# One scatter for four experts through rotating row blocks, in a two-layer expert kernel with a fixed TensorE order

## The chip, the cores and the metric

The kernel runs on one core of a Trainium2 chip, as one program. The metric is the device time of one execution, in microseconds (us); lower is better. All arithmetic on activations and weights is in float32, some of it as pairs of reduced-precision halves.

The engines by their short names: PE (TensorE) multiplies matrices into PSUM, its accumulation memory, and PEld is its weight load; DVE (VectorE) and ACT (ScalarE) do elementwise work; SP (SyncE) issues the transfers. Each engine takes its instructions in the order in which they stand in its queue.

## The reference

Two layers over 256 latent tokens and 256 context tokens of width 1024. In each, a mixer (attention, windowed attention, short convolution), and then 16 routed experts of which each picks its own 32 tokens of each stream. In the second layer only the latent stream goes on to the experts.

```python
def expert_choice_ffn(h, w_router, w_g, w_u, w_d):
    B, n, D = h.shape
    cap = CAPACITY_FACTOR * n // N_EXPERTS                  # 32
    logits = jnp.einsum('bnd,de->ben', h, w_router, preferred_element_type=jnp.float32)
    aff = jax.nn.softmax(logits, axis=1)
    gate, idx = lax.top_k(aff, cap)
    bi = jnp.arange(B)[:, None, None]
    xs = h[bi, idx]
    a = jnp.einsum('becd,edf->becf', xs, w_g)
    u = jnp.einsum('becd,edf->becf', xs, w_u)
    y = jnp.einsum('becf,efd->becd', jax.nn.silu(a) * u, w_d)
    return jnp.zeros_like(h).at[bi, idx].add(y * gate[..., None].astype(y.dtype))

def reference(...):
    for l in range(DEPTH):                                  # 2
        ...
        x = x + gt1 * latent_mixer(...)
        h2 = modulate(rmsnorm(x, g_ffn[l]), sh2, sc2)
        x = x + gt2 * expert_choice_ffn(h2, w_router[l], w_e_gate[l], w_e_up[l], w_e_down[l])
        ...                                                 # the same for the context stream, not in the last layer
    return x
```

## The kernel before

Weights are streamed. `Arena` holds 21 slots of 1 MB (128 partitions x 2048 float32). Loads stand in one queue in the order of `load_mixer` and `load_experts`; SP issues each into the slot that was given back longest ago, and waits there until the last reader of that slot is done. `limit` caps how many tiles may be loaded and not yet used up. An expert has 12 such tiles: `("g", l, e, q)` and `("u", l, e, q)` for the gate and up weights of rows 256 q and on, q from 0 to 3, and `("d", l, e, q)` for the down weights. Expert 15's come in halves of 512 KB.

`experts(l, last, lg)` runs one layer's experts; `last` is layer 1. The number of streams `ns` is 2 in layer 0 and 1 in layer 1, so an expert has NC = 64 rows in layer 0 (32 of each stream) and 32 in layer 1. Routing leaves `pos` (for each token and expert its slot number from 1 to 32, or 0) and the gates (`PA[:, 1]`). Then, expert by expert:

- `gather(g)` builds the one-hot tile `OH` of experts 4g to 4g+3 and multiplies the tokens by it (tile `xg` in PSUM); ACT and DVE bring it to `XS`, modulated. It is called once for four experts, at e = 4g - 2.
- `gate_up(e, q)` multiplies XS by the gate and up tiles into two `gu` tiles in PSUM. In layer 0 each matmul fills 64 columns of the array, and a gate matmul and an up matmul that stand next to each other lie in its two halves; in layer 1 four lie beside each other.
- ACT copies the `gu` tiles out, PE transposes them (`guT`), ACT and DVE make `aT` = silu(gate) x up.
- `down` multiplies aT by the down tiles into `py`, in row blocks of 32, and DVE multiplies `py` by the residual gate into `ys`.
- `spread(e)` builds the way back, `SP`: a matmul (`sp`) copies the expert's row of slot numbers and gates to all partitions, and DVE compares it with the slot number of each partition.
- The scatter (`sc`) multiplies SP by ys, and DVE adds the result to the stream X. In layer 0 it follows every second expert: two experts share the 128 rows, with two partial sums for each of their 64-row blocks. In layer 1 one expert fills all 128 rows with four partial sums, and the scatter follows every expert.

A scheduler sets the order of each engine's instructions from the program's dependencies and its own cost estimates, on PE too. PSUM buffers: four `mm` (gu, guT, sp), one `tp`, one `po`, and one `ps` of two banks (py, and xg of the later gathers).

Of the kernel before, what the change touches and what calls it, by code (L numbers as in the profile page):

```python
# [23 lines left out]
NE = 16  # L24
HID = 1024
CAP = 32
# [63 lines left out]
def hybrid_kernel(ctx, tc, x, c, cx, c_ctx, w_ada, b_ada, g_mix, g_ffn, w_in, qg_a, kg_a, qg_b, kg_b, sink_b,  # L90
# [149 lines left out]
    slotid = const.tile([128, 1], F32, name="slotid")  # L240
    scr = epool.tile([128, CAP], F32, name="scr")
    DVE.scalar_tensor_tensor(scr, slots, 1.0, sel2, op0=OP.mult, op1=OP.mult, accum_out=slotid)
# [772 lines left out]
    def experts(l, last, lg):  # L1015
# [15 lines left out]
        PA = pool.tile([64, 2, 256], F32, name="PA")  # L1031
# [33 lines left out]
        DVE.tensor_tensor(out=av, in0=av, in1=sm.unsqueeze(3).to_broadcast(full), op=OP.mult)  # L1065
        gap(True)
# [23 lines left out]
        def gather(g, mid=None):  # L1090

            if last:

                i, XS = None, gtt[l, 2][1][:, 0].rearrange("p (d e c) -> p d e c", d=8, e=4) if g % 2 else \
                    pool.tile([128, 8, 4, NC], F32, name="XS", tag="XS", bufs=1)
            else:
                i, XS = ar.take([128, 8, 4, NC], F32, "XS")
            XG[g] = (i, XS)

            OH = pool.tile([128, 2 * ns, 4, CAP], F32, name="OH", tag="OH", bufs=1)  # L1100
            for t in tiles:
                DVE.tensor_tensor(out=OH[:, t], in0=pos[:, t, 4 * g:4 * g + 4].unsqueeze(2).to_broadcast([128, 4, CAP]),
                                  in1=slots.unsqueeze(1).to_broadcast([128, 4, CAP]), op=OP.is_equal)
                if g == 0:

                    ACT.activation(OH[:, t], OH[:, t], AF.Copy, scale=nst[:, 3, t:t + 1])
            for h in range(2):
                for s in range(ns):
                    pt = (ptp, ppo)[(h + s) % 2]([128, 4, 128], "xg") if g == 0 else pss([128, 4, 128], "xg")
                    for j in range(4):  # L1110
                        for t in range(2):
                            PE.matmul(pt[:, j, :], (Y if g else X)(2 * s + t)[:, feats(4 * h + j)],  # L1112
                                      OH[:, 2 * s + t].rearrange("p e c -> p (e c)"), start=(t == 0), stop=(t == 1))
                    for j in range(4):
                        d = 4 * h + j
                        o, i_ = XS[:, d, :, 32 * s:32 * s + 32], pt[:, j, :].rearrange("p (e c) -> p e c", e=4)
                        a, b = mod[:, l, 3, s, d:d + 1], mod[:, l, 2, s, d:d + 1]
                        if j % 2:
                            DVE.tensor_scalar(o, i_, a, b, op0=OP.mult, op1=OP.add)  # L1119
                        else:  # L1120
                            ACT.activation(o, i_, AF.Identity, scale=a, bias=b)
                if h == 0 and mid:
                    mid()

        def spread(e):

            se = pool.tile([64, 128], F32, name="se", tag="af", bufs=1)
            n = 128 // ns
            for s in range(ns):
                DVE.tensor_copy(se[0:NR, n * s:n * s + n],  # L1130
                                ident[0:NR, 32 * place(e, s) + e:32 * place(e, s) + e + 1].to_broadcast([NR, n]))
            ps = pmm([128, 512], "sp")
            PE.matmul(ps, se[0:NR], PA[0:NR].rearrange("p a n -> p (a n)"), start=True, stop=True)  # L1133
            af = pool.tile([128, 256], F32, name="af", tag="af", bufs=1)
            ACT.activation(af, ps[:, 256:512], AF.Copy)  # L1135
            if e % ns == 0:
# [174 lines left out]
```

## Time and profile before

| | |
|---|---|
| median of three runs | 1847.61 us (1846.89 to 1850.54) |
| the profiled execution | 1850.58 us, of which the profile's span is 1848.8 |
| mean granted TensorE clock | 0.983 |
| PE busy over the span | 1699.3 us (92%) |
| DVE, ACT busy | 773.6 (42%), 500.5 (27%) |
| bytes moved | 533.79 MB, mean 289 GB/s |
| layer 0's experts | from 556.2 to 1084.3 us |
| layer 1's experts, first gate and up matmuls on | from about 1403 us to the end |

The profiled execution lies 3 us above the median, so a sum made against its span is carried over to the median as a difference. Busy time of PE includes the drain of each run of matmuls, so matmuls that lie beside each other in the array are counted once. The chain of waits follows the work that ended last back from the end: each row is a start, a length and what ran; "issue" is a small gap at the start of an instruction. A matmul in float32 stands as two records, and some records are missing from a trace. The share of DMA is the mean busy share of the 16 DMA engines.

### The profile page before, as it was taken

Reading aid. Unit: us, or ns where it says so; the run is one execution under the profiler, and the core shown is the slowest. Engines: PE = TensorE matmul, PEld = TensorE weight load, DVE = VectorE, ACT = ScalarE, POOL = GpSimd, SP = SyncE. Lnnn points to the kernel's source line nnn. Section 1 sums busy time; section 2 is a strip of 40 time slices with the busy share of each in tenths; the row PEclk is TensorE's granted clock in tenths of the full one; section 3 lists DMA queues with packets and bytes.
Section 4 is the critical chain, followed back from the end, with each engine's and each line's share of the span. In section 5 each row is a group of like instructions: output and inputs, shape, how many; then the busy total and the mean of one; then the engine's idle time right before and its main releaser. Section 6 shows DMA issues by size and latency. Waiting matters only on the chain.

```text
span 1848.8 us, 23239 instructions
## 1 busy us (share of the span) xinstructions
PE 1699.3 (92%) x9198; PEld 935.9 (51%) x9198; DVE 773.6 (42%) x1766; ACT 500.5 (27%) x1089; POOL 0.6 (0%) x6
## 2 busy tenths in 40 slices
PE   7999999999999999899899989999999987778776
PEld 4886666778764333433433337878973322112111
DVE  4787864344542231231221256987653221212111
ACT  4564543223322101101101055655542000000000
POOL 0000000000000000000000000000000000000000
PEclk9999999999999999999999999999999999989999
DMA  9201116655878979989789992235788999999998
GB/s 345 99 27 45 49 66 220 218 166 160 318 294 340 420 294 420 383 362 419 311 359 419 408 365 86 92 92 161 229 337 351 419 420 419 420 420 419 420 420 340
DMA packets 131777, 533.79 MB, mean 289 GB/s; under 512 B 12452, under 2 KB 21076, under 8 KB 85588
## 3 DMA queue, kind: packets, MB, share of 16 engines
q1 hardware_dynamic: 129024, 529.90, 74.0%
q10 hardware_dynamic: 2644, 2.40, 0.4%
q8 instruction: 73, 1.20, 0.3%
q14 instruction: 36, 0.29, 0.0%
HBM read 531.21 MB, written 1.05 MB: 288 GB/s over the span
## 4 chain that ended last, share of the span: by engine, by line
PE 70%; DMA 23%; DVE 3%; ACT 2%; issue 1%; ACTq 0%; SPq 0%; DVEq 0%
DMA s<-in_w_e_up_dram 15%; PE gu L1163 14%; DMA s<-in_w_e_down_dram 8%; PE pf L436 7%; PE pf L437 7%; PE pf L438 7%; PE py L1227 7%; PE sc L1254 3%; PE O L834 3%; PE xg L1112 2%; PE S L772 2%; PE ada L303 2%; PE PTp L808 2%; PE pt L436 2%; PE pt L438 2%; PE pt L437 2%
## 5 line engine op out<-in xcount | busy, mean ns | idle before, releaser
L1163 PE MATMUL gu<-s,s 128*64 128x512 f32 (+1 forms) x1536 | 341.1, 602 | 26.1 <-DMA s<-in_w_e_up_dram 20.8
L437 PE MATMUL pf<-s,wh 128*128 128x512 f32 (+1 forms) x768 | 263.2, 343 | 0.0
L436 PE MATMUL pf<-s,wh 128*128 128x512 f32 (+1 forms) x768 | 262.1, 342 | 0.0
L438 PE MATMUL pf<-s,wl 128*128 128x512 f32 (+1 forms) x768 | 261.6, 342 | 0.0
L467 DVE TENSOR_TENSOR wl<-s,wh 128x512 fp32r<-128x512 f32 x272 | 186.1, 688 | 156.4 <-ACT wh L466 138.2
L466 ACT ACTIVATE wh<-s 128x512 fp32r<-128x512 f32 x272 | 170.5, 630 | 276.3 <-PE pf L437 189.5
L1227 PE MATMUL py<-s,aT 128*32 128x512 f32 x1536 | 200.1, 616 | 33.1 <-DMA s<-in_w_e_down_dram 14.9
L1163 PEld LDWEIGHTS gu<-s,s 128*64 128x64 f32 (+1 forms) x1536 | 99.8, 127 | 249.3 <-issue 182.6
L436 PEld LDWEIGHTS pf<-s,wh 128*128 128x128 f32 x768 | 145.4, 189 | 22.7 <-issue 5.2
L1245 DVE TENSOR_TENSOR ys<-py,s 64x512 f32<-64x512 f32 (+1 forms) x96 | 64.8, 688 | 212.2 <-PE py L1227 201.7
L438 PEld LDWEIGHTS pf<-s,wl 128*128 128x128 f32 x768 | 145.3, 190 | 14.9 <-issue 1.8
L437 PEld LDWEIGHTS pf<-s,wh 128*128 128x128 f32 x768 | 145.6, 190 | 13.9 <-issue 0.7
L1254 PE MATMUL sc<-ys,SP 128*128 128x512 f32 x256 | 124.6, 618 | 17.8 <-DVE ys L1245 17.6
L1227 PEld LDWEIGHTS py<-s,aT 128*32 128x32 f32 x1536 | 52.0, 112 | 159.2 <-issue 95.7
L1213 DVE TENSOR_TENSOR aT<-aT,guT 128x256 f32<-128x256 f32 x48 | 20.0, 420 | 257.1 <-ACT aT L1212 256.6
L1186 ACT ACTIVATE gu<-gu 128x512 f32<-128x512 f32 x48 | 28.5, 596 | 348.4 <-PE gu L1163 348.4
L1135 ACT ACTIVATE af<-sp 128x256 f32<-128x256 f32 x32 | 12.2, 382 | 403.5 <-PE sp L1133 403.5
L1257 DVE TENSOR_TENSOR s<-s,sc 128x512 f32<-128x512 f32 x128 | 87.8, 687 | 37.6 <-PE sc L1254 37.3
L1254 PEld LDWEIGHTS sc<-ys,SP 128*128 128x128 f32 x256 | 40.9, 188 | 104.2 <-DVE s L1257 47.7
L1163 PE MATMUL gu<-s,XS 128*32 128x512 f32 x512 | 80.9, 627 | 11.2 <-DMA s<-in_w_e_up_dram 9.2
L1140 DVE SCALAR_TENSOR_TENSOR SP<-sp,slotid,af 64x256 f32<-64x256 f32 (+1 forms) x48 | 23.2, 484 | 140.0 <-ACT af L1135 139.7
L1112 PE MATMUL xg<-OH,s 128*128 128x128 f32 x384 | 58.3, 309 | 17.7 <-DVE s L1119 14.1
(203 smaller groups left out, 1854.1 us busy)
## 6 DMA issues: line engine op xcount, KB each, us to landing
s<-in_w_e_gate_dram SPq DMA_DIRECT2D x120, 1024.0 KB, 19.0
s<-in_w_e_up_dram SPq DMA_DIRECT2D x120, 1024.0 KB, 16.5
s<-in_w_e_down_dram SPq DMA_DIRECT2D x120, 1024.0 KB, 15.2
s<-in_w_ada_dram SPq DMA_DIRECT2D x48, 1024.0 KB, 10.9
s<-in_w_in_dram SPq DMA_DIRECT2D x46, 1024.0 KB, 7.9
s<-in_w_branch_dram SPq DMA_DIRECT2D x16, 512.0 KB, 10.3
s<-in_w_out_dram SPq DMA_DIRECT2D x8, 1024.0 KB, 7.6
s<-in_w_e_gate_dram SPq DMA_DIRECT2D x16, 512.0 KB
```

The lines of the kernel that those rows point to most:

```text
L436: PE.matmul(ps, lh, rh, start=start, stop=False)
L437: PE.matmul(ps, lh, rl, start=False, stop=False)
L438: PE.matmul(ps, ll, rh, start=False, stop=stop)
L466: ACT.activation(hi, w[:, kk, :], AF.Copy)
L467: DVE.tensor_tensor(out=lo, in0=w[:, kk, :], in1=hi.bitcast(F32), op=OP.subtract)
L834: PE.matmul(O[64 * kv:64 * kv + 64], v[:, k0 + kt, c0:c0 + 64], ipt[kv][1][:, kt].rearrange("p g q -> p (g q)"), start=(kt == 0), stop=(kt ...
L1112: PE.matmul(pt[:, j, :], (Y if g else X)(2 * s + t)[:, feats(4 * h + j)], OH[:, 2 * s + t].rearrange("p e c -> p (e c)"), start=(t == 0), ...
L1163: PE.matmul(gps[fh % nf][r0:r0 + NC], XG[e // 4][1][:, k, e % 4, :], w[a][:, k % 2, 512 * fh:512 * fh + 512], start=(k == 0), stop=(k == 7))
L1227: PE.matmul(py[r0:r0 + 32, h, :], aT[:, ff, 32 * s:32 * s + 32], rhs, start=(ff < n // 32), stop=(ff >= 8 - n // 32))
L1245: DVE.tensor_tensor(out=ys[place(e, i)][r, hs_], in0=py[r, h, :], in1=g2[place(e, i)][r, hs_], op=OP.mult)
L1254: PE.matmul(po[s], back["now"][s][:, ts_], ys[s][:, hs_], start=True, stop=True)
L1257: DVE.tensor_tensor(out=o, in0=o, in1=po[s], op=OP.add)
```

## The change

In layer 0, four experts share one scatter. `block(e, s, h)` = (e + s + 2h) mod 4 names the row block of 32 in which expert e of a group of four has its rows of stream s for half h of the width. `down` in layer 0 goes over both halves and both streams for each 128-row slice of the hidden dimension, so that four neighbouring matmuls have four row blocks; each block now holds one whole sum, and both halves of an expert lie in one bank of `py` (bank e mod 2). `evac` brings the four blocks to `ys`, and `scatter` runs once for four experts, after the last gate and up matmul of the next expert; in layer 1 it runs after that of the next expert too, once for each expert.

`spread` and its matmul are gone. In layer 0 `one_hot` also makes `OG`, the one-hot times the gates with its first three experts repeated, and `way_back` transposes four-expert windows of it on PE, one window for each of two halves and four token tiles; in layer 1 it builds the gated one-hot `four` of one expert and transposes that.

The gather is split in halves, in two alternating PSUM buffers (`tp`, `po`). `gate_up` takes `ks`, so that half of a tile pair can be multiplied: two of the four k-slices' matmuls of the next expert's first pair stand before `guT` and two after it. The load queue has that first pair ahead of this expert's down tiles. In the expert loop PE's instructions stand in the order of the program (`manual_schedule`); the other engines' order stays with the scheduler.

PE in layer 0, around the scatter of a pair of experts before (gu: gate and up matmuls with their weight tile and XS, py: down, sc: scatter; the numbers are those of buffers):

```order
L1227 MATMUL py<-s_4834,aT 32x512 x8
L1163 MATMUL gu<-s_4854,s_4638 64x512
L1163 MATMUL gu<-s_4844,s_4638 64x512
L1254 MATMUL sc_4984<-ys,SP 128x512
L1254 MATMUL sc_4983<-ys,SP 128x512
L1163 MATMUL gu<-s_4854,s_4638 64x512
L1163 MATMUL gu<-s_4844,s_4638 64x512
L1254 MATMUL sc_4989<-ys,SP 128x512
L1254 MATMUL sc_4990<-ys,SP 128x512
L1254 MATMUL sc_4997<-ys,SP 128x512
```

Here gate and up matmuls of the next expert stand one by one between the scatter's. And PE in layer 0 now, around the scatter of the first four experts, which stands in expert 4:

```order
L1183 MATMUL gu<-s_5182,s_5025 64x512
L1216 MATMUL sc<-ys,SP 128x512 x8
L1183 MATMUL gu<-s_5192,s_5025 64x512
L1183 MATMUL gu<-s_5194,s_5025 64x512
L1183 MATMUL gu<-s_5192,s_5025 64x512
L1183 MATMUL gu<-s_5194,s_5025 64x512
L1275 MATMUL guT<-ident,gu 128x128 x8
L1183 MATMUL gu<-s_5192,s_5025 64x512
L1183 MATMUL gu<-s_5194,s_5025 64x512
L1183 MATMUL gu<-s_5192,s_5025 64x512
L1183 MATMUL gu<-s_5194,s_5025 64x512
L1308 MATMUL py<-s_5224,aT 32x512 x8
```

The scatter has moved behind this expert's own gate and up matmuls, the next expert's first pair stands on both sides of guT, and gate and up alternate without a break.

PE at the end of layer 1 (expert 15) before:

```order
L1163 MATMUL gu<-s_12163,s_7303 32x512
L1209 MATMUL guT<-ident,gu 128x128 x4
L1227 MATMUL py<-s_12166,aT 32x512 x4
L1227 MATMUL py<-s_12177,aT 32x512 x4
L1254 MATMUL sc_12297<-ys,SP 128x512
L1254 MATMUL sc_12301<-ys,SP 128x512
```

The transposes follow the last gate and up matmul. The same place now, with OGT the transposed one-hot of `way_back`:

```order
L1183 MATMUL gu<-s_11941,s_7097 32x512
L1216 MATMUL sc<-ys,SP 128x512 x4
L1156 MATMUL OGT<-ident,four 128x128 x2
L1275 MATMUL guT<-ident,gu 128x128 x4
L1232 MATMUL py<-s_11944,aT 32x512 x4
L1232 MATMUL py<-s_11955,aT 32x512 x4
L1216 MATMUL sc<-ys,SP 128x512 x2
```

Expert 14's scatter and expert 15's two transposes have come between the last gate and up matmul and guT. The diff, cut to its core:

```diff
     def load_experts(l):
+        def up(e, q):
+            for nm, w in (("g", w_e_gate), ("u", w_e_up)):
+                rows((nm, l, e, q), w[l, e], q, 2 if e == NE - 1 else 1)
+
+        up(0, 0)
         for e in range(NE):
 
             parts = 2 if e == NE - 1 else 1
-            for q in range(4):
-                for nm, w in (("g", w_e_gate), ("u", w_e_up)):
-                    rows((nm, l, e, q), w[l, e], q, parts)
+            for q in range(1, 4):
+                up(e, q)
+            if e + 1 < NE:
+                up(e + 1, 0)
...
+        aff = pool.tile([128, 2 * ns, NE], F32, name="aff")
+        DVE.tensor_copy(aff.rearrange("p (s t) e -> p t s e", t=2), av)
...
+        def one_hot(g):
...
+            OG = None if last else pool.tile([128, 4, 7, CAP], F32, name="OG", tag="OG", bufs=1)
+            hot[g] = (OH, OG)
...
+            for b0, n in () if last else ((0, 4), (4, 3)):
+                DVE.tensor_tensor(out=OG[:, :, b0:b0 + n], in0=OH[:, :, 0:n],
+                                  in1=aff[:, :, 4 * g:4 * g + n].unsqueeze(3).to_broadcast([128, 2 * ns, n, CAP]),
+                                  op=OP.mult)
...
+        def gather(g, h):
+            OH, XS = hot[g][0], XG[g][1]
+            for s in range(ns):
+                pt = (ptp, ppo)[(h + s) % 2]([128, 4, 128], "xg")
...
+        def block(e, s, h):
+            return (e + s + 2 * h) % 4
+        def way_back(e):
+            if last:
+                pt = ptp([128, 2, 128], "OGT")
+                four = pool.tile([128, 2, 4, CAP], F32, name="four", tag="four", bufs=1)
+                for t in range(2):
+                    DVE.scalar_tensor_tensor(four[:, t], slots.unsqueeze(1).to_broadcast([128, 4, CAP]),
+                                             pos[:, t, e:e + 1],
+                                             aff[:, t, e:e + 1].unsqueeze(2).to_broadcast([128, 4, CAP]),
+                                             op0=OP.is_equal, op1=OP.mult)
+                    PE.transpose(pt[:, t, :], four[:, t].rearrange("p e c -> p (e c)"), ident)
+                back[e] = pool.tile([128, 2, 128], F32, name="SP", tag="SP", bufs=2)
+                ACT.activation(back[e], pt, AF.Copy)
+                return
+            OG = hot[e // 4][1]
+            back[e // 4] = pool.tile([128, 2, 4, 128], F32, name="SP", tag="SP", bufs=1)
             for h in range(2):
+                pt = (ptp, ppo)[h]([128, 4, 128], "OGT")
+                for t in tiles:
+                    o = block(0, 4 - t // 2, -h) % 4
+                    PE.transpose(pt[:, t, :], OG[:, t, o:o + 4].rearrange("p e c -> p (e c)"), ident)
+                ACT.activation(back[e // 4][:, h], pt, AF.Copy)
...
-        def spread(e):
...
+        def gate_up(e, q, ks=(0, 1)):
...
+        def evac(e, py, h):
+            hs_ = slice(512 * h, 512 * h + 512)
+            if last:
+                DVE.tensor_tensor(out=ys[0][:, hs_], in0=py[:, h, :], in1=g2[0][:, hs_], op=OP.mult)
+                return
+            for s in range(ns):
+                r = slice(32 * block(e, s, h), 32 * block(e, s, h) + 32)
+                DVE.tensor_tensor(out=ys[s][r, hs_], in0=py[r, e % 2, :], in1=g2[s][r, hs_], op=OP.mult)
+
+        def scatter(e, h):
+            hs_ = slice(512 * h, 512 * h + 512)
+            for t in range(2):
+                for s in range(ns):
+                    po = (ptp, ppo)[(s if ns == 2 else t)]([128, 512], "sc")
+                    w = back[e][:, t] if last else back[e // 4][:, h, 2 * s + t]
+                    PE.matmul(po, w, ys[s][:, hs_], start=True, stop=True)
+                    o = X(2 * s + t)[:, hs_]
+                    DVE.tensor_tensor(out=o, in0=o, in1=po, op=OP.add)
...
+        order = tc.manual_schedule(engines={mybir.EngineType.PE})
+        order.__enter__()
         for e in range(NE):
...
+            if e and (last or e % 4 == 0):
+                scatter(e - 1, 0)
+                scatter(e - 1, 1)
+            if last or e % 4 == 1:
+                way_back(e)
+            if last or e % 4 == 0:
                 ys = [pool.tile([128, D], F32, name="ys", tag=f"ys{s}", bufs=1) for s in range(ns)]
-            if e + 1 < NE:
-                spread(e + 1)
-            if e % 4 == 2 and e + 2 < NE:
-                gather(e // 4 + 1)
+            ahead = e % 4 == 2 and e + 2 < NE
+            if ahead:
+                one_hot(e // 4 + 1)
+                gather(e // 4 + 1, 0)
...
+            if e + 1 < NE:
+                gate_up(e + 1, 0, (0,))
...
+            if ahead:
+                gather(e // 4 + 1, 1)
+            if e + 1 < NE:
+                gate_up(e + 1, 0, (1,))
+            if last or e % 2 == 0:
+                py = pss([128, 2, 512], "py")
...
+                for q in range(4):
+                    w = ar.get(("d", l, e, q))
                     for ff in range(2 * q, 2 * q + 2):
+                        for h in range(2):
+                            for s in range(ns):
+                                r0 = 32 * block(e, s, h)
+                                PE.matmul(py[r0:r0 + 32, e % 2, :], aT[:, ff, 32 * s:32 * s + 32],
+                                          w[:, ff % 2, 512 * h:512 * h + 512], start=(ff == 0), stop=(ff == 7))
+                    ar.done(("d", l, e, q))
...
-                                square(X, 2 * s + t, h)
+                evac(e, py, h)
+                if e == NE - 1:
+                    scatter(e, h)
+        order.__exit__(None, None, None)
```

More of the change, by code (lines that the diff above doesn't have):

```diff
@@ L1087, in experts @@
             DVE.tensor_copy(pos[:, 2 * s:2 * s + 2, :], pt[:, :, 32 * s:32 * s + NE])
-        def gather(g, mid=None):
+        XG, hot = {}, {}
+        def one_hot(g):
             if last:
@@ L1125, in spread @@
-        def spread(e):
[L1127 to L1136, printed above, removed]
-                back["next"] = [pool.tile([128, 256], F32, name="SP", tag=f"SP{s}", bufs=2) for s in range(ns)]
-            for s in range(ns):
-                r = slice(n * s, n * s + n)
-                DVE.scalar_tensor_tensor(back["next"][place(e, s)][r], ps[r, 0:256], slotid[r], af[r],
-                                         op0=OP.is_equal, op1=OP.mult)
@@ L1158, in gate_up @@
             w = [ar.get(key) for key in keys]
-            for k in range(2 * q, 2 * q + 2):
+            for k in (2 * q + i for i in ks):
                 for fh in range(2):
@@ L1173, in experts, with down @@
         g2 = [gtt[l, 5][1][:, s, :] for s in range(ns)]
-        spread(0)
         ar.limit(LIMIT[l][3])
+        ys, halves = None, False
+        def evac(e, py, h):
[8 more added lines that the diff above has]
+            hs_ = slice(512 * h, 512 * h + 512)
+            for t in range(2):
+                for s in range(ns):
[5 more added lines that the diff above has]
+                    if e == NE - 1:
+                        if last:
+                            nc.sync.dma_start(out=out[0, 128 * t:128 * t + 128, hs_], in_=o)
+                        else:
+                            square(X, 2 * s + t, h)
+        def down(e, py, h, qs):
+            for q in qs:
+                w = ar.get(("d", l, e, h, q // 2) if halves else ("d", l, e, q))
+                for ff in range(2 * q, 2 * q + 2):
+                    rhs = w[:, ff % 4, :] if halves else w[:, ff % 2, 512 * h:512 * h + 512]
+                    r0 = 32 * (ff % 4)
+                    PE.matmul(py[r0:r0 + 32, h, :], aT[:, ff, :], rhs, start=(ff < 4), stop=(ff >= 4))
+        order = tc.manual_schedule(engines={mybir.EngineType.PE})
+        order.__enter__()
         for e in range(NE):
@@ new lines, in experts @@
+            if ahead:
[4 more added lines that the diff above has]
+                py = pss([128, 2, 512], "py")
+            halves = (l, e) == (DEPTH - 1, NE - 1)
+            if halves:
+                for h in range(2):
+                    for i in range(2):
+                        down(e, py, h, (2 * i, 2 * i + 1))
+                        ar.done(("d", l, e, h, i))
+                    evac(e, py, h)
+                    scatter(e, h)
+                continue
@@ new lines, in experts @@
+            if last:
+                for q in (0, 2):
+                    for h in range(2):
+                        down(e, py, h, (q, q + 1))
+                    for i in (q, q + 1):
+                        ar.done(("d", l, e, i))
+            else:
+                for q in range(4):
+                    w = ar.get(("d", l, e, q))
+                    for ff in range(2 * q, 2 * q + 2):
+                        for h in range(2):
+                            for s in range(ns):
[3 more added lines that the diff above has]
+                    ar.done(("d", l, e, q))
```

106 lines of the change are left out of this document (29 added, 77 removed).

## The prediction

> **What bounds the kernel now.** I read first the busy time of each engine by stage (columns: stretch, its length, busy time and count of PE, PEld, DVE, ACT, POOL, then granted TensorE clock, DMA share, GB/s). The four stretches are layer 0 up to its first expert's gather, layer 0's experts, layer 1's mixer with its routing, layer 1's experts.
>
> ```profile
> 0.00:556.20 556.20, 541.00 (x2749) 393.74 (x2750) 318.16 (x787) 233.91 (x520) 0.56 (x6) 0.99 0.49 168
> 556.20:1084.30 528.10, 503.76 (x2599) 191.94 (x2601) 135.95 (x267) 61.61 (x135) 0.00 (x0) 0.99 0.92 376
> 1084.30:1409.80 325.50, 311.30 (x2043) 251.85 (x2046) 231.10 (x553) 174.31 (x373) 0.00 (x0) 0.98 0.56 188
> 1409.80:1848.80 439.00, 343.23 (x1818) 98.38 (x1810) 88.35 (x160) 30.71 (x65) 0.00 (x0) 0.97 1.00 411
> ```
>
> Layer 1's experts are bound by the weight stream (DMA share 1.00, PE at 343 of 439): PE work taken out there buys nothing. Layer 0's experts are bound by PE, but not by much: PE idles 24.3 us of 528 and the stream is already at 0.92. So a gain in PE time counts until the stream is full. Next, the chain of waits in layer 0, which gives the price of each step and shows what PE waits for.
>
> ```profile
> 572.97 7.02 PE gu L1163 x32
> ...
> 638.03 2.09 PE xg L1112 x16
> ...
> 642.14 2.14 PE xg L1112 x16
> ...
> 682.31 0.69 DVE ys L1245
> 683.01 0.04 issue
> 683.05 1.98 PE sc L1254 x4
> 685.04 1.00 PE gu L1163 x2
> 686.04 5.73 PE sc L1254 x12
> ...
> 699.64 1.05 PE sp L1133 x2
> ...
> 733.28 0.60 ACT gu L1186
> ...
> 733.90 0.39 ACT aT L1212
> ...
> 734.31 0.43 DVE aT L1213
> ...
> 734.79 7.12 PE py L1227 x64
> ...
> 744.65 1.00 PE gu L1163 x2
> ```
>
> A matmul stands as two records. From one "gu x2" to the next (685.04 to 744.65) two experts take 59.6 us. The work priced by these rows: gate and up 64 records, 14.0 us; down 7.1; one spread 1.05; a pair's scatter 1.98 + 5.73 = 7.7. The transposes, 8 to an expert, come from the groups of the same stage:
>
> ```profile
> L1254 PE MATMUL sc<-ys,SP 128*128 128x512 f32 x128 | 62.3, 618 | 5.9 <-DVE ys L1245 5.6 <-DVE s L1257 0.2
> L1112 PE MATMUL xg<-OH,s 128*128 128x128 f32 x256 | 37.1, 303 | 12.1 <-DVE s L1119 12.1
> L1209 PE MATMUL guT<-ident,gu 128*128 128x128 f32 x128 | 22.7, 305 | 1.8 <-ACT gu L1186 1.1
> L1133 PE MATMUL sp<-PA,se 64*128 64x512 f32 x32 | 18.0, 641 | 0.0
> ```
>
> That is 22.7 / 128 = 0.18 us a record, 2.8 us an expert (an upper price, since a group's busy time counts each run's drain). Last, what the stream has to spare:
>
> ```profile
> 580.00:590.00 10.00, 10.00 (x58) 3.72 (x62) 2.01 (x6) 5.25 (x9) 0.00 (x0) 1.00 0.44 143
> 590.00:1057.00 467.00, 444.88 (x2280) 166.53 (x2273) 119.22 (x230) 42.90 (x94) 0.00 (x0) 0.99 0.92 380
> 650.00:660.00 10.00, 10.00 (x58) 4.18 (x59) 3.26 (x11) 1.30 (x3) 0.00 (x0) 1.00 0.00 0
> 920.00:930.00 10.00, 7.05 (x44) 3.69 (x48) 1.23 (x3) 1.29 (x3) 0.00 (x0) 0.66 0.00 0
> 1500.00:1510.00 10.00, 8.35 (x46) 2.22 (x40) 0.42 (x1) 0.98 (x2) 0.00 (x0) 0.70 1.01 419
> ```
>
> and where it ends: the last issues of layer 0 on SP's queue, and the median time to landing of such halves.
>
> ```profile
> 1040.51 9.45 SPq L68 DMA_DIRECT2D s<-in_w_e_down_dram  x8
> s<-in_w_e_down_dram SPq DMA_DIRECT2D x16, 512.0 KB, 10.3
> ```
>
> A full stream moves 419 GB/s (1500 to 1510, in layer 1). From 590 to 1057 it moves 380, so it stands still for 467 x (1 - 380/419) = 43.5 us, in lumps at the gathers (nothing at all from 650 to 660 and 920 to 930): the slots are full and wait for PE. Layer 0's last weights are issued by 1049.7 and land 10.3 later, about 1060.
>
> **The change, part by part, in layer 0.**
> Scatters: 32 matmuls instead of 64. 32 x 0.96 us (7.7 / 8) = 30.8 us off PE; 32 DVE adds go with them, beside PE's work.
> Spreads: 16 go, 16 x 1.05 = 16.8 us. In their place PE transposes a gated one-hot, 8 transposes for four experts, 32 in all: 64 records x 0.18 = 11.5 us at most. Their ACT evacuations (two per group of four experts) and two more DVE products per group lie under gate and up matmuls, where DVE is busy 136 us of the stage's 528 and ACT 62.
> PE's waits: the gather blocks wait out each evacuation from one buffer (640.12 to 642.14: 2.0 us each, 12.1 in the stage). They now alternate between two buffers, with half an expert's first gate and up tiles and the transposes between the halves. The wait for gu, aT and down (0.60 + 0.39 + 0.43 us in the rows from 733.28) gets four gate and up matmuls, 1.75 us, ahead of the transposes and as many behind. The scatter comes a full gate and up later than its ys. I take 20 of the 24.3 us as gone; what stays is the end, where nothing is left to put in between.
> Whole pairs: a lone gate or up matmul takes 1.00 us (685.04), as long as two that run side by side in the two column halves (7.02 / 8 = 0.88). The old order strews such single ones between scatters; the new one keeps them in pairs. This is the gap between 59.6 us and the priced 2 x (14.0 + 7.1 + 2.8 + 1.05) + 7.7 = 57.6, less 1.5 of waits: about 0.5 us an interval, 4 in all.
> Down matmuls: the same 32, still four row blocks of 32 in turn, so 7.1 us as before; not shown is that the four now share one accumulation bank for both halves of the width. Bounds: 0, or one by one as the scatter runs, far off; I take 0, since four blocks shared a bank before too. The ys operations stay four of 512 columns per expert.
> PE's need falls by 30.8 + 16.8 - 11.5 + 20 + 4 = 60 us: PE alone would end the stage at 1024.
> The stream: the queue loads the next expert's first pair ahead of this one's down weights, in the order in which PE now takes them; both versions reuse a slot after the same 14 to 17 tiles. The stream can be full from 590 on, which puts its last landing 43.5 us earlier, at 1016.5. The one-hot's first chain has 128x512 and 128x384 products more (0.69 + 0.52 us by the ys row) before PE starts, so slots come free 1.2 us later: 1017.7. Behind the last landing PE has a quarter of the down work, 1.8 us, and the end of the stage, 1084.3 - (1075.5, end of py) = 8.8. That makes 1028.3. The later of the two bounds counts: the stage ends 56 us earlier, bound by the stream, with PE some 4 us short of it and so often waiting for weights.
>
> The Trainium skill, "DMA: Bandwidth & Descriptors", Specifications, gives about 358 GB/s of HBM bandwidth to a core. By it the stage's 201 MB would be an estimated 562 us, more than the stage takes now, and the change could gain nothing; the trace's 419 decides against it.
>
> **In layer 1.** The start of the mixer follows the stage, and its first conditioning weights are issued right behind the last expert weights:
>
> ```profile
> 1053.28 21.43 SPq L68 DMA_DIRECT2D s<-in_w_ada_dram  x8
> 1084.31 1.90 PE ada L303 x16
> ```
>
> They come 43 us earlier while PE comes 56 earlier. The first is now issued 31 us ahead of its use (1053.28 to 1084.31); 18 remain, more than the 10.3 that down halves took to land. I cost it at 0. In the stream-bound experts PE saves 16 spreads and adds 32 transposes, to no effect. At the very end, order matters:
>
> ```profile
> 1830.39 1.09 PE gu L1163 x6
> ...
> 1832.21 0.76 PE guT L1209 x4
> ...
> 1837.66 1.98 PE sc L1254 x4
> ```
>
> PE is in order. Expert 14's scatter, four matmuls (2 x 1.98 = 4.0 us), and two transposes (0.76 by the guT row, an equal number of records to it) now stand between the last gate and up matmul, released by the last landing, and guT. They cover the 0.73 us wait for ACT's copy. That adds 4.0 + 0.8 - 0.7 = 4.1 us; a part comes back, since the last down weights have landed by then. I take +3.5 (bounds 0, if the scatter ran in an earlier wait after all, and +5).
>
> **Sum.** -56 + 3.5 = -52.5 us against the profiled execution (span 1848.8, time 1850.58); the median of the runs is 1847.61, so 1795.
>
> **Rivals.**
> PE stays the bound, at a lower clock. In layer 1, where PE waits for weights, the clock is 0.97 in the mean and 0.70 from 1500 to 1510; after the wait at 920 it is 0.66. If the new waits do that in layer 0, PE's 468 us (528 - 60) at 0.95 are 493, and the stage ends at 1049: 1816. Against it: PE waits only at the margin, in pieces of 1 or 2 us, and between the gathers the clock held 1.00. The Trainium skill, "TensorE: Matmul & The Clock Gate", on HAM oscillation, says that a wait over about 3.4 us halves the clock for the next window; no row here shows such waits in layer 0.
> A larger gain: if PE frees slots early enough to fill 580 to 590 too (6.6 us lost there) and the tail costs nothing: 1785.
> Slower: the stream stops. The next expert's first pair is now held across the transposes, 2.8 us longer. If the slots run out on this, the stream halts that long at each of 32 experts, 90 us: 1885. It decides at 52.5 / 32 = 1.6 us each. Against it: 14 or 15 slots stand against the 12 tiles of an expert, and layer 1 at 411 GB/s has no lead to lose.
> No change: the stream is at its limit already and stands still for another reason than PE. Against it: its stops lie at the gathers, where PE idles.
>
> **Chances.** Stream-bound as summed 0.64, own range 1787 to 1803; PE or clock bound 0.22, 1803 to 1830; larger gain 0.08; slower 0.04; no change 0.02. A measurement of this kernel tells about 0.2% from nothing, so faster 0.94, same 0.02, slower 0.04. The range reaches from the larger gain to most of the clock case: 1784 to 1822.
>
> **What would show it.** Right: scatter records in layer 0 halve to 64, no spreads, DMA share near 1 from 590 to about 1018, PE in layer 0 waiting for w_e_down and w_e_up instead of DVE, the stage's end at about 1028, all of layer 1 shifted by 56 with its expert stage the same length but for 3 or 4 us at the end. Wrong: a clock under 0.96 in the stage, stream gaps at experts' ends, or down matmuls longer than 7.1 us an expert.

## The result and the profile after

The changed kernel takes 1791.13 us (median of four runs, 1789.51 to 1793.91) against 1848.74 for the kernel before in the same comparison: a ratio of 0.969, 95% interval 0.9673 to 0.9707. The prediction was 1795. The profiled execution took 1791.10, its span is 1789.4. Layer 0's experts and the two stages behind them (columns as in the prediction's first view; the last two rows are pieces of layer 0's experts):

```profile
556.40:1024.30 467.90, 438.62 (x2534) 165.73 (x2538) 99.88 (x182) 61.79 (x130) 0.00 (x0) 1.00 1.00 413
1024.30:1343.90 319.60, 304.77 (x1996) 249.64 (x1997) 229.78 (x550) 172.09 (x367) 0.00 (x0) 0.98 0.59 205
1343.90:1789.40 445.50, 345.24 (x1865) 94.70 (x1864) 87.31 (x164) 32.29 (x68) 0.00 (x0) 0.96 0.99 408
...
580.00:590.00 10.00, 9.47 (x62) 3.32 (x60) 0.75 (x2) 6.50 (x11) 0.00 (x0) 1.00 0.73 272
...
590.00:1014.00 424.00, 398.23 (x2328) 147.27 (x2320) 85.26 (x152) 44.31 (x92) 0.00 (x0) 1.00 1.01 420
```

Layer 0's experts end 60.0 us earlier (1024.3 against 1084.3; they also begin later, so that the stage itself is 62.6 shorter); all later stages together give back 0.6, which makes the span's 59.4. From 590 to the last landing the stream does not stop: 420 GB/s at a share of 1.01, where it had 380. The groups of PE in that stage and, below them, what PE waited for between 590 and 1010 (total, times, longest):

```profile
L1183 PE MATMUL gu<-s,s 128*64 128x512 f32 x1024 | 241.7, 598 | 24.5 <-DMA s<-in_w_e_up_dram 21.8 <-DMA s<-in_w_e_gate_dram 2.0 <-ACT s L1137 0.5
L1308 PE MATMUL py<-s,aT 128*32 128x512 f32 x1024 | 114.2, 594 | 2.4 <-DMA s<-in_w_e_down_dram 1.6 <-DVE aT L1279 0.5
L1128 PE MATMUL xg<-OH,s 128*128 128x128 f32 x256 | 32.3, 284 | 0.5 <-ACT OH L1119 0.4
L1216 PE MATMUL sc<-ys,SP 128*128 128x512 f32 x64 | 31.0, 618 | 1.1 <-DVE ys L1208 0.8 <-DVE s L1218 0.2
L1275 PE MATMUL guT<-ident,gu 128*128 128x128 f32 x128 | 19.9, 297 | 0.1
L1166 PE MATMUL OGT<-ident,OG 128*128 128x128 f32 x32 | 4.4, 279 | 0.0
```

```profile
PE gu L1183 <- DMA s<-in_w_e_up_dram: 21.8, 19, 1.5
PE gu L1183 <- DMA s<-in_w_e_gate_dram: 2.0, 4, 0.6
PE py L1308 <- DMA s<-in_w_e_down_dram: 1.6, 4, 0.5
```

The waits for DVE and ACT are all but gone (2.4 us are left in the stage) and waits for weights stand in their place, none longer than 1.5 us. The chain of waits at the stage's end runs through the stream:

```profile
993.56 10.38 DMA s<-in_w_e_up_dram
1003.96 10.28 DMA s<-in_w_e_down_dram
...
1014.28 1.11 PE py L1308 x8
...
1020.37 3.90 PE sc L1216 x8
```

The last down weights land at 1014.2; 10.0 us of work that nothing covers follow. So the stage is bound by the stream, as forecast. How far PE lies below that bound, a busy PE does not tell: that was the first question for the experiments.

### The profile page after: what moved, and what is told of

Read it like the earlier page. It is cut to its first block, busy times and chain, and to the rows that moved or that the text cites. A ratio compares the mean times of both kernels' runs of the same rounds, so it can differ in the third digit from the quotient of the medians.

```text
span 1789.4 us, 23088 instructions
## 1 busy us (share of the span) xinstructions
PE 1630.0 (91%) x9134; PEld 904.0 (51%) x9134; DVE 734.8 (41%) x1678; ACT 499.3 (28%) x1081; POOL 0.6 (0%) x6
## 4 chain that ended last, share of the span: by engine, by line
PE 54%; DMA 40%; DVE 3%; ACT 2%; issue 1%; SPq 0%; ACTq 0%; DVEq 0%
DMA s<-in_w_e_up_dram 29%; DMA s<-in_w_e_down_dram 11%; PE pf L439 7%; PE pf L440 7%; PE pf L441 7%; PE gu L1183 5%; PE O L837 3%; PE S L775 2%; PE ada L306 2%; PE PTp L811 2%; PE pt L439 2%; PE pt L441 2%; PE pt L440 2%; PE py L1308 2%; PE xg L1128 1%; PE sc L1216 1%
## 5 line engine op out<-in xcount | busy, mean ns | idle before, releaser
L1183 PE MATMUL gu<-s,s 128*64 128x512 f32 (+1 forms) x1536 | 336.4, 616 | 66.9 <-DMA s<-in_w_e_up_dram 54.6
L1183 PEld LDWEIGHTS gu<-s,s 128*64 128x64 f32 (+1 forms) x1536 | 89.5, 128 | 281.1 <-issue 135.6
L1218 DVE TENSOR_TENSOR s<-s,sc 128x512 f32<-128x512 f32 x96 | 65.9, 687 | 258.1 <-PE sc L1216 258.1
L1232 PE MATMUL py<-s,aT 128*32 128x512 f32 x512 | 83.8, 632 | 23.4 <-DMA s<-in_w_e_down_dram 21.7
L1216 PE MATMUL sc<-ys,SP 128*128 128x512 f32 x192 | 93.4, 619 | 2.8 <-DVE ys L1204 1.7
L1208 DVE TENSOR_TENSOR ys<-py,s 32x512 f32<-32x512 f32 x64 | 44.0, 687 | 126.5 <-PE py L1308 125.7
L1308 PEld LDWEIGHTS py<-s,aT 128*32 128x32 f32 x1024 | 31.2, 110 | 83.3 <-issue 71.9
L439 PE MATMUL pt<-wh,s 128*128 128x512 f32 x160 | 65.1, 407 | 1.7 <-ACT s L497 1.7
L441 PE MATMUL pt<-wh,s 128*128 128x512 f32 x160 | 65.2, 407 | 0.0
L1216 PEld LDWEIGHTS sc<-ys,SP 128*128 128x128 f32 x192 | 30.6, 189 | 68.3 <-DVE s L1218 35.4
```

Source lines behind the costliest of these rows:

```text
L439: PE.matmul(ps, lh, rh, start=start, stop=False)
L441: PE.matmul(ps, ll, rh, start=False, stop=stop)
L1183: PE.matmul(gps[fh % nf][r0:r0 + NC], XG[e // 4][1][:, k, e % 4, :], w[a][:, k % 2, 512 * fh:512 * fh + 512], start=(k == 0), stop=(k == 7))
L1208: DVE.tensor_tensor(out=ys[s][r, hs_], in0=py[r, e % 2, :], in1=g2[s][r, hs_], op=OP.mult)
L1216: PE.matmul(po, w, ys[s][:, hs_], start=True, stop=True)
L1218: DVE.tensor_tensor(out=o, in0=o, in1=po, op=OP.add)
```

## Experiments

In the table all times are medians in us; "stage" is the length of layer 0's experts in the profiled run, from the first gather's first matmul to the last scatter's last. Runs with the same letter share their runs of the kernel before (1849.65, 1850.03 and 1847.81 for A, B and C).

| run | | median | ratio to before, interval | stage |
|---|---|---|---|---|
| before | | 1848.74 | | 528.2 |
| after | | 1791.13 | 0.969 (0.9673 to 0.9707) | 465.6 |
| short_stream | A | 1751.02 | 0.9467 (0.9451 to 0.9483) | 426.8 |
| before_short_stream | A | 1807.45 | 0.9772 (0.9757 to 0.9786) | 485.8 |
| double_scatter | A | 1794.59 | 0.9707 (0.9692 to 0.9721) | 471.8 |
| free_order | A | 1796.08 | 0.9713 (0.9697 to 0.9729) | 472.2 |
| after_again | B | 1791.40 | 0.9674 (0.964 to 0.9709) | 465.6 |
| tail | B | 1789.84 | 0.9668 (0.9633 to 0.9702) | 465.4 |
| head | B | 1789.34 | 0.966 (0.9622 to 0.9698) | 466.0 |
| head_tail | B | 1787.72 | 0.9655 (0.9621 to 0.9689) | 466.1 |
| before_two_buffers | C | 1830.22 | 0.9901 (0.988 to 0.9922) | 508.3 |
| old_load_order | C | 1797.54 | 0.9725 (0.9704 to 0.9746) | 470.9 |
| free_short | C | 1756.33 | 0.9497 (0.9471 to 0.9522) | 434.0 |
| free_double | C | 1821.52 | 0.9855 (0.9834 to 0.9877) | 498.8 |

**How much room PE has: short_stream.** The changed kernel with three of four down tiles of layer 0 not loaded (the first serves for all four), so that the stream is a quarter shorter there and PE's own need shows.

```diff
-                for q in range(4):
+                for q in range(4 if l else 1):
...
-                    w = ar.get(("d", l, e, q))
+                    w = ar.get(("d", l, e, 0))
```

> The changed kernel, but layer 0 loads one down tile per expert instead of four and uses it for all four (the layer-0 down product is therefore another one; PE does the same matmuls). The stream of layer 0 falls from 192 to 144 tiles, about 120 us, so PE alone decides when the stage ends. Theory 1, the changed stage is bound by the stream and PE has some 20 us to spare (transposes are one record each, so they were priced twice too high): stage ends at about 1004, time 1771. Theory 2, PE and stream are level as the prediction had it (PE alone 1024): time 1787 or more. Theory 3, PE in its fixed order is itself the bound: 1791, no change.

40 us faster than the changed kernel, twice the 20 us of theory 1. PE is busy for all but 2.4 us of the stage and waits for no weight:

```profile
L1183 PE MATMUL gu<-s,s 128*64 128x512 f32 x1024 | 229.0, 596 | 0.5 <-ACT s L1137 0.5
L1308 PE MATMUL py<-s,aT 128*32 128x512 f32 x1024 | 113.2, 594 | 0.6 <-DVE aT L1279 0.5
L1128 PE MATMUL xg<-OH,s 128*128 128x128 f32 x256 | 32.3, 284 | 0.5 <-ACT OH L1119 0.4
L1216 PE MATMUL sc<-ys,SP 128*128 128x512 f32 x64 | 31.0, 619 | 1.0 <-DVE ys L1208 0.8 <-DVE s L1218 0.2
```

The transposes (guT, OGT) take 19.9 and 4.4 us as in the changed kernel. PE's need is 426.8 us where the prediction had 468 (528 - 60): PE lies 38.8 us below the stream, not 4. In the changed kernel these stand as 24 us of waits for weights and as 12.7 us in gu's busy time (241.7 against 229.0: a gate matmul whose up tile has not landed runs without its partner).

**The same in the kernel before: before_short_stream.**

```diff
-                for q in range(4):
+                for q in range(4 if l else 1):
...
-                    w = ar.get(("d", l, e, h, q // 2) if halves else ("d", l, e, q))
+                    w = ar.get(("d", l, e, h, q // 2) if halves else ("d", l, e, q if last else 0))
```

> The kernel before, with the same cut: one down tile per expert of layer 0 loaded and used four times (another layer-0 down product). Theory 1, the kernel before is bound by PE in layer 0 throughout: time unchanged, 1848 within 4. Rival, its stage already waits on the stream in places (after the gathers, where the stream had stood still): 5 to 15 us less. The difference to the changed kernel with the same cut is what the change takes out of PE's path when no stream limits it: theory 1 says about 77, theory 2 about 60.

It became 42 us faster, which neither expectation has, though PE waited for no weight in the kernel before. The run does not tell what it was made for, since with fewer loads the scheduler wrote PE another order: the gate and up matmuls that run without a partner in the trace (no record of another one starts within 0.2 us of theirs; lone ones from here on) fall from 59 to 32, and PE's 24.4 us of waits to 1.1. Two groups of it:

```profile
L1163 PE MATMUL gu<-s,s 128*64 128x512 f32 x1024 | 245.4, 598 | 0.0
...
L1112 PE MATMUL xg<-OH,s 128*128 128x128 f32 x256 | 33.8, 287 | 0.0
```

So some 40 of the 528 us were not work that has to be done: 23.3 of waits, 9.3 in gu, 8.1 at xg, guT and py.

**The scatters put back as load: double_scatter.** Every scatter matmul of layer 0 runs twice (the sum is taken from the second).

```diff
-                    PE.matmul(po, w, ys[s][:, hs_], start=True, stop=True)
+                    for _ in range(1 if last else 2):
+                        PE.matmul(po, w, ys[s][:, hs_], start=True, stop=True)
```

> The changed kernel with each of layer 0's 32 scatter matmuls issued twice into the same buffer (same result): 32 x 0.96 = 30.6 us of PE work are put back, nothing else. Theory 1 (PE has some 20 us to spare under the stream): about 10 us more, 1801. Theory 2 (4 us to spare): 27 us more, 1818. Theory 3 (PE is the bound): 31 us more, 1822.

```profile
L1183 PE MATMUL gu<-s,s 128*64 128x512 f32 x1024 | 235.9, 597 | 13.1 <-DMA s<-in_w_e_up_dram 12.0 <-ACT s L1137 0.5 <-DMA s<-in_w_e_gate_dram 0.5
...
L1217 PE MATMUL sc<-ys,SP 128*128 128x512 f32 x128 | 56.0, 595 | 0.8 <-DVE ys L1208 0.8
```

+3.5 us, less than any of the three theories has. Of 25 us more scatter, 11.4 fit into gu's waits and 5.8 into its busy time; the last down matmul ends at 1015.3 in both kernels, and only the last scatter, which nothing covers, shows: the stage ends at 1030.1 where the changed kernel has 1024.3. Layer 1's mixer was 3.3 us shorter in this run; no run shows why. Halving the scatter matmuls, the largest named part of the change, is therefore worth 3.5 us of the time, 5.9 at the stage's end, once the rest is there.

**The order by itself: free_order, free_short, free_double.** The written order of PE is taken out: alone, with the short stream (three of four down tiles of layer 0 not loaded), and with the doubled scatters.

```diff
-        order = tc.manual_schedule(engines={mybir.EngineType.PE})
-        order.__enter__()
...
-        order.__exit__(None, None, None)
```

> The changed kernel with the fixed TensorE order taken away in both layers, so that the scheduler orders PE as it does in the kernel before; all else is the same. Theory 1 (fewer matmuls do most, the order's whole pairs and covered waits are worth 15 to 30 us of PE time, of which the 20 us to spare take the most): 0 to 10 us more, 1791 to 1801. Theory 2 (only 4 us to spare): 11 to 26 us more, 1802 to 1817. If the order matters for nothing: 1791.

> The changed kernel without the written TensorE order, and with one down tile an expert in layer 0 used for all four (three quarters of layer 0's down weights are not loaded). PE is the bound here, so this prices the order when the stream does not cover it. Theory 1 (the written order saves PE the lone halves of gate and up pairs): 12 to 20 us slower than the changed kernel with the same short stream, 1763 to 1771, with gate and up taking 240 us or more of PE against 229. Rival (order without a loaded stream costs nothing, the scheduler keeps pairs too): within 4 us of it, 1749 to 1755.

> The changed kernel without the written TensorE order and with each scatter matmul of layer 0 run twice: the two savings undone together that cost 5 and 3.5 us each alone. Theory 1 (each alone only uses up PE's 39 us of room; together they pass it, since without the order PE is busy for the whole stage): 20 to 30 us slower than the changed kernel, 1811 to 1821, no idle time on PE. Rival (without the order PE's busy time is waiting in disguise, lone halves paced by arriving weights): the two costs add, 7 to 10 us, 1798 to 1801.

The same two groups of free_order, of free_double, and gu of free_short:

```profile
L1183 PE MATMUL gu<-s,s 128*64 128x512 f32 x1024 | 270.9, 598 | 0.0
...
L1216 PE MATMUL sc<-ys,SP 128*128 128x512 f32 x64 | 33.3, 628 | 3.5 <-DVE ys L1208 3.3 <-DVE s L1218 0.2
```

```profile
L1183 PE MATMUL gu<-s,s 128*64 128x512 f32 x1024 | 270.0, 599 | 0.0
...
L1217 PE MATMUL sc<-ys,SP 128*128 128x512 f32 x128 | 60.8, 610 | 3.3 <-DVE ys L1208 3.3
```

```profile
L1183 PE MATMUL gu<-s,s 128*64 128x512 f32 x1024 | 236.4, 597 | 0.0
```

free_order is 5 us slower than the changed kernel and waits for no weight, yet gu takes 270.9 us of PE: 91 gate and up matmuls are lone in its trace, none in short_stream's, which has the written order and waits for no weight either. Is that PE's time, or waiting in disguise? free_double answers: 1821.5, or 25.4 us over free_order, where the rival's added costs (5 and 3.5) gave 1798 to 1801; theory 1 had 1811 to 1821. PE is the bound there, busy for 494.2 of the stage's 498.8 us, and the lone matmuls are work that counts. free_short fits neither expectation: 5.3 us slower than short_stream, with gu at 236.4 and 15 lone matmuls, so that this price of the order lies between the two theories. Over five orders in which PE waits for no weight, gu's busy time grows with the number of lone matmuls:

| | short_stream | free_short | before_short_stream | before | free_order |
|---|---|---|---|---|---|
| lone matmuls of 512 | 0 | 15 | 32 | 59 | 91 |
| gu busy, us | 229.0 | 236.4 | 245.4 | 254.7 | 270.9 |

From 0 to 59 it is 25.7 us, from 0 to 91 it is 41.9: 0.44 and 0.46 us for each (0.50 and 0.51 in the two between), about half of the 0.88 us that a pair takes. The changed kernel, with 21 lone ones where the second tile of a pair came late, is left out, since its gu waits for weights.

**The gather's waits by themselves: before_two_buffers.** One edit in the kernel before.

```diff
-                    pt = (ptp, ppo)[(h + s) % 2]([128, 4, 128], "xg") if g == 0 else pss([128, 4, 128], "xg")
+                    pt = (ptp, ppo)[(h + s) % 2]([128, 4, 128], "xg")
```

> The kernel before with one edit: the gathers after the first rotate between two accumulation buffers, as the changed kernel's do. Theory 1 (before is bound by PE, and the 12.1 us that PE waits for the evacuation of the gather blocks lie on its path): 10 to 13 us faster than before, 1835 to 1838, with the idle time before xg near 0 and the stage about 516 us. Rival (the waits only move: PE meets the same lateness at the scatter or at full slots): 0 to 4 us faster, with idle time grown before sc or py.

```profile
L1227 PE MATMUL py<-s,aT 128*32 128x512 f32 x1024 | 113.2, 594 | 1.5 <-DVE aT L1213 0.6
...
L1112 PE MATMUL xg<-OH,s 128*128 128x128 f32 x256 | 33.2, 286 | 1.0 <-DVE s L1119 1.0
```

17.6 us faster (stage -19.9), more than the 10 to 13 expected: 11.1 us of waits before xg and 3.1 before py (which the profile puts down to no engine) are gone, and xg and py are busy for 5.6 less (33.2 against 37.1, 113.2 against 114.9). Most of this last part is the clock. PE in the kernel before at layer 0's last gather, with its waits in brackets:

```profile
911.52 3.28 PE L1112 MATMUL xg<-OH,s 128*128 128x128 f32 x16 [1.36 <-DVE s L1119]
916.82 2.12 PE L1112 MATMUL xg<-OH,s 128*128 128x128 f32 x16 [2.02 <-DVE s L1119]
920.97 2.63 PE L1112 MATMUL xg<-OH,s 128*128 128x128 f32 x16 [2.02 <-DVE s L1119]
925.57 8.84 PE L1227 MATMUL py<-s,aT 128*32 128x512 f32 x64 [1.98 <-issue]
```

The same 16 records of xg take 2.12 us at the full clock, the 64 of py 7.07. The granted clock is 0.53 from 912 to 914 and 0.50 from 926 to 928, and one xg run of the gather near 780 takes 3.44: together 4.8 us over the full clock. In before_two_buffers no run of xg or py is that slow, and the clock is 1.00 in the stage. This rotation is part of the change; it was worth 17.6 us by itself where PE was the bound.

**The order of the loads: old_load_order.** The changed kernel, with PE's written order left as it is and all four pairs of an expert loaded ahead of its down weights.

```diff
-            for q in range(1, 4):
+            for q in range(0 if e else 1, 4):
                 up(e, q)
-            if e + 1 < NE:
-                up(e + 1, 0)
```

> The changed kernel with the weight loads issued in the order of the kernel before (all four up and gate pairs of an expert ahead of its down weights, none of the next expert's). Theory 1 (the order of loads matters little, since the slots hold more than one expert's tiles): 0 to 2 us slower than the changed kernel, 1790 to 1794. Rival (the first pair loaded early is what keeps PE supplied between the experts): 4 to 10 us slower, 1795 to 1801, with PE waiting for w_e_up or w_e_gate at each expert's start and the stream under 415 GB/s.

The time is the rival's (1797.5, its runs 1796.8 to 1799.3 against 1789.5 to 1794.1 of the changed kernel), but the mechanism is neither's: the stream stays full, at 419 GB/s from 590 to 1020, and PE's waits in the stage come to about as much as in the changed kernel. What differs is their length, the clock behind them and the work that is left behind the last one. The stage and a piece of it, then PE's instructions with their idle time in brackets:

```profile
560.60:1031.50 470.90, 444.94 (x2532) 166.45 (x2535) 97.82 (x178) 61.26 (x129) 0.00 (x0) 0.97 1.00 413
...
720.00:722.00 2.00, 2.00 (x6) 0.41 (x2) 0.00 (x0) 0.00 (x0) 0.00 (x0) 0.50 1.01 422
```

```profile
716.65 1.04 PE L1181 MATMUL gu<-s,s 128*64 128x512 f32 x2 [3.51 <-DMA s<-in_w_e_gate_dram]
719.04 3.67 PE L1181 MATMUL gu<-s,s 128*64 128x512 f32 x6 [1.35 <-DMA s<-in_w_e_up_dram]
...
778.70 3.29 PE L1181 MATMUL gu<-s,s 128*64 128x512 f32 x6 [1.36 <-DMA s<-in_w_e_up_dram]
...
897.13 1.04 PE L1181 MATMUL gu<-s,s 128*64 128x512 f32 x2 [1.25 <-DMA s<-in_w_e_gate_dram]
899.52 1.93 PE L1181 MATMUL gu<-s,s 128*64 128x512 f32 x6 [1.35 <-DMA s<-in_w_e_up_dram]
...
986.84 1.46 PE L1181 MATMUL gu<-s,s 128*64 128x512 f32 x2 [3.30 <-DMA s<-in_w_e_gate_dram]
989.31 3.68 PE L1181 MATMUL gu<-s,s 128*64 128x512 f32 x6 [1.00 <-DMA s<-in_w_e_up_dram]
992.92 1.69 PE L1273 MATMUL guT<-ident,gu 128*128 128x128 f32 x8
```

The next expert's first pair now stands behind the down weights in the stream and ahead of down in PE's order, so PE waits for it with the down work queued behind. After a wait of 3.51 us six records take 3.67 us at half the clock. After waits of 1.25 and 1.35 us with one matmul between them they take 1.93, but after 1.24 and 1.36 us at 778.70 they took 3.29. Four waits of 3.30 to 3.84 us were each followed by the half clock. The Trainium skill, "TensorE: Matmul & The Clock Gate", on HAM oscillation, gives idle gaps over about 3.4 us as the danger; the traces here have the half clock behind shorter ones too, behind 3.30 us in this run and behind waits of 1.36 to 2.02 us in the kernel before. The stage's mean clock falls from 1.00 to 0.97 and PE's busy time rises from 438.6 to 444.9.

That is not yet the stage's 5.3 us. What PE loses ahead of a wait for the stream it makes up in that wait, since the stream does not slow down. The last weights are as late as the stage's start, 2.0 us (the last eight down issues run from 997.0 to 1006.2, in the changed kernel from 995.0 to 1004.3), so the 5.3 us lie behind them: from the last wait, which ends at 989.3, PE has 42 us of unbroken work, expert 14's down and all of expert 15. The half clock in it is an estimated 2.2 us (3.68 against 1.93, and guT 1.69 against 1.22); the rest would be the down work that the wait held up. The 2.0 us before the stage begins (560.6 against 558.6) lie in code that is the same: among the other runs of the changed kernel that leave this code alone, the start is anywhere from 557.5 (after_again) to 560.3 (free_short).

**The ends: after_again, tail, head, head_tail.** In tail, expert 14's scatter and expert 15's way back stand between the last gate and up pairs, and expert 15's scatters behind its last down matmul; in head, the gated copy `OG` and the Y copies of the first expert stand behind what PE waits for; head_tail has both.

```diff
             for q in range(2 if e == 0 else 1, 4):
                 gate_up(e, q)
+                if end and q < 3:
+                    scatter(e - 1, q - 1)
+                    if q == 2:
+                        way_back(e)
...
+            raw = OH if last or g else OG[:, :, 0:4]
...
-                    ACT.activation(OH[:, t], OH[:, t], AF.Copy, scale=nst[:, 3, t:t + 1])
+                    ACT.activation(OH[:, t], raw[:, t], AF.Copy, scale=nst[:, 3, t:t + 1])
```

> The changed kernel itself, beside the three edits below on the same chip. All theories: 0.969 of the kernel before, about 1791.

> The changed kernel with the end of layer 1 put in another order: expert 14's scatter halves stand behind the second and third gate and up tile pairs of expert 15, its two transposes too, ahead of the last pair; and expert 15's second down half stands ahead of its first scatter. Theory, the rows of the changed kernel's chain (scatter 3.82 and transposes 0.36 us between the last gate and up matmul and guT, 0.86 us of wait for ys): 1.5 to 3 us less than the changed kernel, the rest held up by the last down tile's landing. Rival: the last landing alone sets the end, 0 to 0.5 us less.

> The changed kernel with two edits at the start of each layer's experts: the first group's one-hot is scaled before it is multiplied by the gates (DVE's 1.08 us leave the path to the first gather), and the copies of the normalized tokens come after the first expert's silu instead of ahead of it (ACT 4.3 us with the function table's load). Theory, slots come free earlier and the stream, which stands still for 4 to 5 us between 560 and 590, fills up: 2 to 4 us less in layer 0, and as much in layer 1 at most 1. Rival: the slots' count and not PE's progress limits the stream there: no change.

> Both edits together. If they add up: 4 to 7 us less than the changed kernel, 1784 to 1787. Rival (neither counts): 1791.

tail gave 1.6 us and head 2.1 against after_again's 1791.40; each is less than the 0.2% that a measurement of this kernel can tell. In head the stretch from 560 to 590 moves 361 GB/s where after_again has 324, 1.1 MB more, or 2.6 us at 420 GB/s: the mechanism is the expected one. Both together gave 3.7, just under the 4 to 7 expected (runs 1786.99 to 1789.43 against 1789.87 to 1794.10): the lowest median here, though the intervals of the two ratios overlap. head_tail's end shows why tail gave no more:

```profile
1768.26 10.66 DMA s<-in_w_e_down_dram
...
1778.97 1.05 PE py L1232 x4
1780.02 3.84 PE sc L1216 x8
```

The end hangs on the last down weights now; work moved off PE there no longer counts.

## Why the prediction was right, and where not

**The bound moved from PE to the stream: shown.** The stage's last weights landed at 1014.2, forecast 1017.7, and 10.0 us follow, forecast 10.6. Of the missing 3.5 us, 3.1 are the stretch from 580 to 590, which the sum left as it was and gave to the rival of a larger gain: it moves 272 GB/s after and 143 before, and 1.29 MB more at 420 GB/s are 3.1 us. The stage began 2.6 us later than before (1.4 in after_again), where the sum had 1.2.

**PE's need: the mis-sized term.** The prediction took 60 us off; the stage's groups of before against those of short_stream, where PE is the bound, give 101.6 (busy and idle time together; the stage itself 101.4). Groups of before that the prediction did not show:

```profile
L1163 PE MATMUL gu<-s,s 128*64 128x512 f32 x1024 | 254.7, 597 | 0.0
L1227 PE MATMUL py<-s,aT 128*32 128x512 f32 x1024 | 114.9, 601 | 4.6 <-issue 3.1 <-DVE aT L1213 0.6
```

| step of the prediction | forecast | measured |
|---|---|---|
| scatters (sc busy, 62.3 to 31.0) | -30.8 | -31.3 |
| spreads out, transposes in (18.0 to 4.4) | -5.3 | -13.6 |
| waits (24.4 to 2.7) | -20 | -21.7 |
| whole pairs (gu busy, 254.7 to 229.0) | -4 | -25.7 |
| xg, guT, py (busy): longer runs 4.5, full clock at the gathers 4.8 | none | -9.3 |

Two terms failed, and by one miscount. A transpose was counted as two records, as a matmul is, but 32 of them left 32 records, 4.4 us, and the 128 transposes of the prediction's own guT row are x128. So guT was priced at 2.8 us an expert where 8 records of 0.18 are 1.4 (its runs take 1.56). That hid the lone matmuls in the very interval from which whole pairs were priced: with 1.4 the priced work there is 54.8 us and not 57.6, the gap to 59.6 less 1.5 of waits is 3.3, and eight such intervals give 26 us, against the 25.7 measured. The interval holds 8 lone matmuls, the stage 59. The group of the whole stage, which the prediction had at hand and did not use for this, said the same: 254.7 us of gu against 16 x 14.0 = 224. The clock at the gathers was the third thing missed, with 0.66 from 920 to 930 in the prediction's own row.

Two rows were read slightly off. SP's last issues end at 1049.96 (1040.51 + 9.45), not at 1049.7; and between 640.12 and 642.14 PE runs guT for 1.11 us, so that this wait is 1.07 and not 2.0. Neither moves the sum.

The error cost nothing, because the stage ends at the later of two bounds and the other one was right. That is luck in PE's term: the margin forecast between the two bounds was 4 us, the error 41, in the harmless direction. It made "PE some 4 us short of the stream" wrong by a factor of ten, so the rival with PE or its clock as the bound got 0.22 where at 0.95 of the clock PE's 427 us would still have been 449, under the stream's 465.6.

**The clock rival.** It did not come in the changed kernel, with 1.00 in the stage. That the clock halves behind waits is shown, in old_load_order and at the gathers of the kernel before, and the prediction's condition (waits over 3.4 us) is too narrow: at those gathers the waits were 1.36 to 2.02 us, with one run of xg between two of them (2.12 us at the full clock). Why the changed kernel is spared is argued and not shown: the loads stand in PE's order, so about the same 24 us of waits fall in pieces of at most 1.5 us, and between two pieces of over 1 us stand at least 3.6 us of work. The prediction named that load order only as what keeps the stream full, which the old order did too.

**The slots** did not run out: no stop of the stream at experts' ends, so the slower rival fell.

**Layer 1.** The mixer stretch to the first gate and up matmul is 0.7 us longer (forecast 0), the experts up to the last up weight's landing 1.6 us shorter, and the tail 1.5 us longer (forecast 3.5):

```profile
1770.46 3.82 PE sc L1216 x8
1774.28 0.36 PE OGT L1156 x2
...
1776.05 1.97 PE py L1232 x16
...
1780.83 1.90 PE py L1232 x16
```

From the last landing to aT's input the chain has 3.1 us more (4.1 forecast; the transposes again cost half). Then 1.6 us come back, where 0.6 were assumed: both halves of down run in 1.97 and 1.90 us, where before they took 3.0 and 2.6:

```profile
1833.89 1.91 PE py L1227 x12
...
1835.82 1.08 PE py L1227 x4
...
1839.65 2.59 PE py L1227 x16
```

So -60.0 + 0.7 - 1.6 + 1.5 = -59.4 in the trace and -57.6 in the medians, against -52.5 forecast.

**What stays open.** before_short_stream changed two things at once, and no run has the order of the kernel before under a shorter stream. No run has old_load_order's loads at the full clock, so how its 5.3 us divide is an estimate. Layer 1's mixer took 316 to 321 us over the runs, from the stage's end to the first gate and up matmul; why was not looked into, and a difference of 3 us between two runs can come from there.

## What to carry to other kernels

Price each kind of work, multiply it up over the stage and set it against the group's total, and check the number of records behind each price: gu's total was 30.7 us above its price, 25.7 of it lone matmuls, while a transpose priced at twice its cost hid them in the interval of the chain. When a change moves the bound from one resource to another, forecast both ends separately; the gain is cut off at the second bound (here 101 us of PE's need became 60 us of time), and parts of the change that look large (half the scatters) are then worth little each. Under a full stream, load in the order in which the engine takes the tiles: not for bandwidth, which was full either way, but so that little work stands behind the last wait and the unavoidable waits come in short pieces.

## What was not expected of the hardware

- Waits of 3.30 to 3.84 us were followed by half the clock (0.50 for some 7 us after the first of them), while 24 us of waits in pieces of up to 1.5 us left it at 1.00 in the changed kernel. No single length divides the two: 1.24 + 1.36 us with one matmul between them had the half clock behind them once, 1.25 + 1.35 did not, and in the kernel before it followed waits of 1.36 to 2.02 us at two of the later gathers.
- A float32 transpose of 128x128 stands as one record where a matmul stands as two: 4.4 us for 32.
- A gate or up matmul of 64 columns without its partner costs PE some 0.45 us more than with it, and this adds up unseen inside busy time: 25.7 us over 59 of them in the kernel before.
- The full stream held 420 GB/s over 424 us with PE busy 94% of the time.
